# GpSimd issues the small loads of a decoder block, two column-pair counts go from 12 and 11 to 14 and 13, and the output projection's second chunk is written ahead of the first sums' eviction

## The chip, the cores and the metric

The kernel runs on one core of one Trainium2 chip. The time is the device time of one execution in microseconds, as the median over several runs; lower is better. The core has a matrix engine (TensorE, "PE", with its weight loads as "PEld"), a vector engine (DVE), a scalar engine (ACT), GpSimd (POOL), and SyncE (SP), which here issues DMAs. Matrix results are written to PSUM (8 banks of 512 float32 columns), everything else lives in SBUF.

## What is computed

One decoder layer over 256 tokens of width 2048, float32 in and out:

```
mod = silu(c) @ w_mod + b_mod          # sh1, sc1, g1, sh2, sc2, g2: 2048 each
h = rmsnorm(x, norm_mix) * (1 + sc1) + sh1
proj = h @ w_in                        # 5660 columns, cut into the inputs of four mixers
y = concat(gla, gated_deltanet, pooling, forgetting_attention)   # 512 columns each
x = x + g1 * (y @ w_out)
h = rmsnorm(x, norm_ffn) * (1 + sc2) + sh2
x = x + g2 * ((silu(conv3(h @ w_gate) + b) * (h @ w_up)) @ w_down)   # 5632 wide inside
out = rmsnorm(x, norm_final)
```

The mixers are sequence models with 4 heads of 128; the gated DeltaNet one has a causal convolution over 4 tokens, small triangular systems and a recurrence over four chunks of 64 tokens.

## The kernel before

**Numbers.** A float32 product is made from three matmuls of rounded parts. A weight tile `wr` (128 x 1024 floats, 512 KB) is loaded by SP (`load`, line 153), ACT rounds it to `wh`, DVE forms the remainder `wl = wr - wh` (`split`, line 114), and PE then multiplies high by high, high by low and low by high. There are five `wr` buffers and three each of `wh` and `wl`.

**Order.** The framework fixes the order of each engine's instructions when the program is built, from a simulated timeline, the order of the program and a few edges written by hand: `tc.issue_after(i)` keeps the instructions of its block behind `i` on the engine of `i`, and `tc.high_priority()` pulls a block forward. On the chip each engine then runs its list strictly in order, and every DMA issue is an instruction in the list of the engine that asks for it.

**Start (lines 289 to 332).** `x` is loaded as `xt`, ACT sums its squares, GpSimd takes the power -1/2, DVE scales both halves of the tokens (`tsc` at line 322), PE transposes 16 column blocks, and ACT copies them to `xnT`.

**Four groups (lines 335 to 527).** The 16 blocks of `h` (128 columns each) are made four at a time. For a group, `mods4` accumulates on DVE the shift and scale rows over 16 tiles `wm` of `w_mod` (512 KB each, five buffers, line 360), then `f` turns them into columns with tiny matmuls, forms `md` (lines 347 to 349), and ACT and DVE write the four blocks of `h`, high and low, into `HL`. While group g is multiplied, the tiles `wm` of group g + 1 are loaded and accumulated, one to a step. Group g's matrix work is `gdn(g)`, six weight tiles for the 1536 DeltaNet columns, summed in six PSUM banks `acc`, and then `extras(g)`: visits to pairs of 128-column blocks. There are 16 such pairs. A visit (`pair`, line 438) multiplies the blocks of `h` that the pair still lacks, four to a weight tile, into a bank `ext`, and adds the sum to `pr`, `gv` or `fv`. `TAKE` says how many pairs groups 0, 1 and 2 visit, counted from the end of the list; what they leave is made up later, so the number of weight tiles is the same for every `TAKE`, and a visit more costs one addition more.

**Small loads.** In group 0, after the third DeltaNet step, `rest` and `small_load` are called: SP issues 13 small loads (norms, biases, convolution weights, the masks' table `ct`) and three loads of `wsm`, 28 single columns of `w_in` as 16, 8 and 4 floats from each of 2048 rows. They stand in SP's list between the weight tiles. `rest` then transposes them, and GpSimd makes 12 masks `mk` from `ct`. `small` (the 28 columns) and `gates` come with group 3.

**Mixers (lines 546 to 943).** The pairs' remaining tiles, paced with loads of further parts of `w_mod` (`bg`: three on PE as `bgt`, three on DVE), are written so that they can run between the small operations of the four mixers, in the order GLA, pooling, attention, DeltaNet. PSUM: `ext` 2 banks, `bgt` 1, `gdt` 2, `oxt` 3.

**Output projection (lines 945 to 989).** Five chunks of columns: 512, 512, 512, 256, 256. `project(n, a)` multiplies one chunk for both halves of the tokens. Chunk 0 goes to the two `ext` banks and is written before `mx.close()`, which gives up the banks of `gdt` and `oxt`; chunks 1 to 4 go to a pool `wot` of five banks made after it. After each chunk DVE and ACT apply g1, the residual and the squares. Then come the feed-forward part (`fpt`) and the output.

Of the kernel before, what the change touches and what calls it, by code (L numbers as in the profile page):

```python
# [47 lines left out]

TAKE = (16, 12, 11)

# [23 lines left out]
def trunk_kernel(ctx: ExitStack, tc: tile.TileContext, x, c, w_mod, b_mod, norm_mix, norm_ffn, w_in,  # L74
# [24 lines left out]
    def tt(o, a, b, op):  # L99
        V.tensor_tensor(out=o, in0=a, in1=b, op=op)  # L100
# [127 lines left out]
    with ExitStack() as ph:  # L228
# [59 lines left out]
        with ExitStack() as st:  # L288
# [31 lines left out]
            G.tensor_tensor(out=ssm[:, 0:2], in0=ssm[:, 2:4], in1=mhalf[:, 0:2], op=ALU.pow)  # L320
            for t in range(NT):
                tsc(xt[:, t], xt[:, t], ssm[:, t:t + 1], None, ALU.mult)
            for k in range(0, KT, 2):
# [11 lines left out]
            def mods(g):  # L335
                for k0 in range(GROUPS[g][0], sum(GROUPS[g]), 4):
                    yield from mods4(k0, min(4, sum(GROUPS[g]) - k0))

            def mods4(k0, nk):
                n = nk * P  # L340

                def f(ga):
                    b = ext()
                    for i in range(2 * nk):
                        mm(b[:, i:i + 1], ga[:, i * P:i * P + P], ones[:, 0:1])
                    md = sp.tile([P, 2 * nk], F32, name="md", tag="md", bufs=2, padded_shape=[P, 16])
                    tt(md[:, 0:nk], b[:, 0:nk], bm(0, k0, nk), ALU.add)
                    tt(md[:, nk:], b[:, nk:2 * nk], bm(1, k0, nk), ALU.add)
                    tt(md[:, nk:], md[:, nk:], nmix[:, k0:k0 + nk], ALU.mult)
                    for kk in range(nk):  # L350
                        k = k0 + kk
                        h = sp.tile([P, T], F32, name="h", tag="h", bufs=2)
                        act(h, xnT[:, k], AF.Identity, scale=md[:, nk + kk:nk + kk + 1], bias=md[:, kk:kk + 1])
                        split(HL[:, k, 0:T], HL[:, k, T:], h)
# [3 lines left out]
                for k in range(KT):  # L358
# [6 lines left out]
                    yield  # L365

            def rest():
                nc.sync.dma_start(wlr[0:16], gla_w_lr[0])
                nc.sync.dma_start(wlr[28:29], gla_b_lr)
                nc.sync.dma_start(r2[0:48], gdn_conv[0].rearrange("j (k p) -> (j k) p", p=P))  # L370
                nc.sync.dma_start(r2[48:52], pool_scale[0].rearrange("(k p) -> k p", p=P))
                nc.sync.dma_start(r2[52:53], gla_norm)
                nc.sync.dma_start(r2[53:54], gdn_norm)
                nc.sync.dma_start(ct, cst[:, P:K_N])
                row = lambda ap: ap.partition_broadcast(P).rearrange("p o h -> p (o h)")
                nc.sync.dma_start(hrow[:, 0:4], row(gdn_a_log))
                nc.sync.dma_start(hrow[:, 4:8], row(gdn_dt_bias))
                nc.sync.dma_start(hrow[:, 8:12], row(fox_f_bias))
                nc.sync.dma_start(r3, ffn_conv_w[0, 0:2].rearrange("j (k p) -> (j k) p", p=P))
                nc.sync.dma_start(r4[0:NF], ffn_conv_w[0, 2].rearrange("(k p) -> k p", p=P))  # L380
                nc.sync.dma_start(r4[NF:], ffn_conv_b[0].rearrange("(k p) -> k p", p=P))
                b = ext()
# [13 lines left out]
            def small_load():  # L396
                nc.sync.dma_start(wsm[:, :, 0:16], wi_v[:, :, C_LR:C_LR + 16])
                nc.sync.dma_start(wsm[:, :, 16:24], wi_v[:, :, C_B:C_B + 8])
                nc.sync.dma_start(wsm[:, :, 24:28], wi_v[:, :, C_FF:C_FF + 4])  # L399
                split(wsh, wsl, wsm)  # L400

            def small():
                o = ext()[0:28, 0:T]
                for k in range(KT):
# [105 lines left out]
            for g in range(NG):  # L510
                nxt = mods(g + 1) if g < NG - 1 else iter(())
                with tc.issue_after(hold[0].ins):
# [3 lines left out]
                    for i, _ in enumerate(gdn(g)):  # L516
                        next(nxt, None)
                        if g == 0 and i == 2:
                            rest()
                            small_load()  # L520
                    if g == NG - 1:
# [3 lines left out]
                for _ in nxt:  # L525
                    pass
                hold[0] = last_wm[0]


# [15 lines left out]

        bgp = ph.enter_context(tc.tile_pool(name="bgp", bufs=1, space=PSUM))
        mx = ph.enter_context(ExitStack())
        gdp = mx.enter_context(tc.tile_pool(name="gdp", bufs=2, space=PSUM, reuse_waits="tile"))
        oxp = mx.enter_context(tc.tile_pool(name="oxp", bufs=3, space=PSUM, reuse_waits="tile"))
        dp = mx.enter_context(tc.tile_pool(name="dp", bufs=1, reuse_waits="tile"))  # L550
# [418 lines left out]

        a0 = [ext(), ext()]  # L970
        project(0, a0)
        mx.close()
        wop = ph.enter_context(tc.tile_pool(name="wop", bufs=5, space=PSUM, reuse_waits="tile"))
        x1 = bigC().rearrange("p (t d) -> p t d", t=NT)
# [3 lines left out]
        with tc.tile_pool(name="op", bufs=2, reuse_waits="tile") as op:  # L978
            for n, (c0, w) in enumerate(chunks):
                ns, gs = slice(c0, c0 + w), slice(c0 % 1024, c0 % 1024 + w)  # L980
                a = a0
                if n > 0:
                    a = [wop.tile([P, 512], F32, name="wot", tag="wot")[:, 0:w] for _ in range(NT)]
                    project(n, a)
# [158 lines left out]
```

## Time and profile before

| | before |
|---|---|
| median of 3 runs | 1299.4 us (1298.0 to 1302.43) |
| the profiled execution | 1305.52 us, of which the span is 1303.7 us |
| PE busy, share of the span | 1247.2 us, 96% |
| DVE, ACT, POOL busy | 888.9, 636.6, 23.5 us |
| read from memory | 308.51 MB |
| feed-forward matmuls (`fpt`) in the chain | 734.96 us, from 553.49 us on |

The span reaches from the first to the last instruction. The page of the profile gives busy times for each engine, the chain of work that ended last (followed back from the end), and the costliest groups of instructions. In a row of the timeline stand start, duration, engine, line, operation, output<-inputs, sizes and how many were merged; in brackets the idle time of the engine before it and what ended it. "SPq" is SP issuing a DMA. In a row of the windows stand, for each engine, busy microseconds and the number of instructions, then PEclk, the granted clock of PE (1.00 is full), the busy share of the DMA engines and their GB/s. Busy times of PE run to a modelled end, so that neighbouring matmuls overlap; how tightly they are packed is read from a stretch's length divided by their number.

### The profile page before, as it was taken

How to read it: one execution, taken by the hardware profiler on the slowest of the kernel's cores; microseconds unless marked ns; L12 is line 12 of the kernel's file. 1: busy time of each engine (PE TensorE's matmuls, PEld its weight loads, DVE VectorE, ACT ScalarE, POOL GpSimd, SP SyncE). 2: the span in 40 equal slices, each digit the busy share in tenths (PEclk: the TensorE clock that was granted, in tenths of full speed). 3: DMA queues.
4: the chain of work that ended last, by engine and by line, in shares of the span. 5: the costliest groups of instructions: out<-in, count | busy, mean ns of one | idle time of the engine just before them, and what ended most of it. 6: DMA issues, size and time to landing. Idle time of an engine off the chain costs nothing.

```text
span 1303.7 us, 19845 instructions
## 1 busy us (share of the span) xinstructions
PE 1247.2 (96%) x7663; PEld 1078.8 (83%) x7663; DVE 888.9 (68%) x1201; ACT 636.6 (49%) x1000; POOL 23.5 (2%) x31
## 2 busy tenths in 40 slices
PE   2799999999999999999999999999999999999995
PEld 1699999898976687888888888888888888888884
DVE  7578797989763387676666656665756687974543
ACT  3455344674364454555555545554555553443432
POOL 0200000010000000000000000000000000000000
PEclk8799999999999999999999999999999999999998
DMA  9999998796557888656666666657666699875662
GB/s 329 270 367 377 320 335 295 250 336 224 174 200 255 311 315 286 176 148 190 180 196 192 180 197 190 190 165 211 190 184 175 208 353 381 306 258 188 194 193 82
DMA packets 168597, 311.91 MB, mean 239 GB/s; under 512 B 16172, under 2 KB 54067, under 8 KB 167863
## 3 DMA queue, kind: packets, MB, share of 16 engines
q1 hardware_dynamic: 168503, 310.65, 72.9%
q8 instruction: 60, 0.98, 0.3%
q14 instruction: 34, 0.28, 0.1%
HBM read 308.51 MB, written 2.10 MB: 238 GB/s over the span
## 4 chain that ended last, share of the span: by engine, by line
PE 91%; DMA 4%; DVE 1%; SPq 1%; ACT 1%; issue 1%; POOLq 0%; ACTq 0%; DVEq 0%
PE fpt L97 56%; PE ext L97 16%; PE wot L97 5%; PE gdt L97 4%; PE acc L97 4%; DMA wm<-in_w_mod_dram 4%; PE bgt L97 3%; PE oxt L97 2%; DMA wr<-in_w_in_dram 1%; DVE ga L103 1%; ACT xT L1011 0%; DVE m L100 0%; DVE wl L100 0%; SPq L399 0%; PE oxt L873 0%
## 5 line engine op out<-in xcount | busy, mean ns | idle before, releaser
L100 DVE TENSOR_TENSOR wl<-wr,wh 128x1024 fp32r<-128x1024 f32 x384 | 469.0, 1222 | 296.8 <-ACT wh L115 296.1
L115 ACT CAST wh<-wr 128x1024 fp32r<-128x1024 f32 x384 | 403.5, 1051 | 490.2 <-PE fpt L97 314.9
L97 PE MATMUL fpt<-bigA,wh 128*128 128x512 f32 x1408 | 399.3, 395 | 2.1 <-DVE bigA L103 2.1
L97 PEld LDWEIGHTS fpt<-bigA,wh 128*128 128x128 f32 x1408 | 239.0, 188 | 32.8 <-issue 2.2
L97 PEld LDWEIGHTS fpt<-bigA,wl 128*128 128x128 f32 x1408 | 222.8, 189 | 34.5 <-DVE wl L100 3.7
L97 PE MATMUL fpt<-bigA,wl 128*128 128x256 f32 x1408 | 240.7, 279 | 0.0
L103 DVE SCALAR_TENSOR_TENSOR ga<-wm,cond,ga 128x1024 f32<-128x1024 f32 x139 | 177.9, 1280 | 14.1 <-DMA wm<-in_w_mod_dram 13.2
L97 PE MATMUL ext<-bigA,wh 128*128 128x256 f32 x768 | 138.4, 282 | 0.0
L97 PE MATMUL fpt<-wl,AH 128*128 128x512 f32 x352 | 137.5, 391 | 0.0
L97 PE MATMUL fpt<-wh,AL 128*128 128x512 f32 x352 | 137.0, 389 | 0.0
L97 PE MATMUL fpt<-wh,AH 128*128 128x512 f32 x352 | 123.4, 390 | 0.0
L97 PEld LDWEIGHTS ext<-bigA,wh 128*128 128x128 f32 x768 | 118.5, 190 | 3.1 <-DVE E L100 0.8
L97 PE MATMUL ext<-bigA,wl 128*128 128x256 f32 x384 | 107.9, 281 | 1.7 <-DVE wl L100 1.7
L97 PEld LDWEIGHTS fpt<-wl,AH 128*128 128x128 f32 x352 | 66.1, 188 | 14.3 <-DVE wl L100 0.4
L97 PEld LDWEIGHTS fpt<-wh,AH 128*128 128x128 f32 x352 | 66.1, 188 | 14.1 <-ACT wh L115 0.2
L97 PEld LDWEIGHTS fpt<-wh,AL 128*128 128x128 f32 x352 | 66.1, 188 | 14.0 <-issue 0.2
L97 PEld LDWEIGHTS ext<-bigA,wl 128*128 128x128 f32 x384 | 72.9, 190 | 2.9 <-DVE wl L100 1.9
L97 PE MATMUL acc<-bigA,wh 128*128 128x256 f32 x384 | 68.7, 285 | 5.6 <-ACT bigA L115 3.2
L97 PE MATMUL ext<-wh,bigA 128*128 128x256 f32 (+1 forms) x320 | 69.3, 308 | 0.0
L97 PEld LDWEIGHTS acc<-bigA,wh 128*128 128x128 f32 x384 | 59.7, 195 | 6.0 <-ACT bigA L115 3.3
L97 PE MATMUL wot<-wh,bigA 128*128 128x512 f32 (+1 forms) x256 | 63.0, 337 | 0.0
L97 PEld LDWEIGHTS ext<-wh,bigA 128*128 128x128 f32 x320 | 52.9, 192 | 5.5 <-issue 1.4
(340 smaller groups left out, 1193.2 us busy)
## 6 DMA issues: line engine op xcount, KB each, us to landing
wm<-in_w_mod_dram SPq DMA_DIRECT2D x192, 512.0 KB, 5.6
wr<-in_w_in_dram SPq DMA_DIRECT2D x88, 512.0 KB, 9.1
wr<-in_ffn_w_gate_dram SPq DMA_DIRECT2D x88, 512.0 KB, 3.7
wr<-in_ffn_w_up_dram SPq DMA_DIRECT2D x88, 512.0 KB, 4.3
wr<-in_ffn_w_down_dram SPq DMA_DIRECT2D x88, 512.0 KB, 4.6
wr<-in_w_out_dram SPq DMA_DIRECT2D x32, 512.0 KB, 4.2
xt<-in_x_dram SPq DMA_DIRECT2D x2, 1024.0 KB, 7.1
bigC<-in_x_dram SPq DMA_DIRECT2D x2, 1024.0 KB, 9.1
```

What stands on the lines that cost most here:

```text
L97: PE.matmul(o, lhsT=l, rhs=r, start=start, stop=stop, skip_group_check=True)
L100: V.tensor_tensor(out=o, in0=a, in1=b, op=op)
L103: V.scalar_tensor_tensor(out=o, in0=a, scalar=s, in1=b, op0=op0, op1=op1)
L115: S_.copy(hi, src)
```

## The change

- `TAKE` is (16, 14, 13) in place of (16, 12, 11).
- The scaling of `xt` goes from two DVE instructions of 2048 columns to four ACT instructions of 1024, both first halves first.
- The 13 loads of `rest` and the three of `small_load` are issued by GpSimd in place of SP, behind the multiplication that finishes `md` of group 1, and that multiplication itself goes from DVE to GpSimd. The rest of `rest` is written after group 2, and the splitting of `wsm` into `small`.
- Output chunk 1 is written before `mx.close()`, into two `oxt` banks, whose pool now stays open; `wot` has two banks, and chunks 2, 3 and 4 use `wot`, `ext` and `oxt`.

```diff
-TAKE = (16, 12, 11)
+TAKE = (16, 14, 13)
...
-            for t in range(NT):
-                tsc(xt[:, t], xt[:, t], ssm[:, t:t + 1], None, ALU.mult)
+            for hs in (slice(0, D // 2), slice(D // 2, D)):
+                for t in range(NT):
+                    act(xt[:, t, hs], xt[:, t, hs], AF.Copy, scale=ssm[:, t:t + 1])
...
-                    tt(md[:, nk:], md[:, nk:], nmix[:, k0:k0 + nk], ALU.mult)
+                    if k0 == GROUPS[1][0]:
+                        asked[0] = G.tensor_tensor(out=md[:, nk:], in0=md[:, nk:], in1=nmix[:, k0:k0 + nk], op=ALU.mult)
+                    else:
+                        tt(md[:, nk:], md[:, nk:], nmix[:, k0:k0 + nk], ALU.mult)
...
+            def rest_load():
+                G.dma_start(wlr[0:16], gla_w_lr[0])
...
             def rest():
-                nc.sync.dma_start(wlr[0:16], gla_w_lr[0])
...
             def small_load():
-                nc.sync.dma_start(wsm[:, :, 0:16], wi_v[:, :, C_LR:C_LR + 16])
-                nc.sync.dma_start(wsm[:, :, 16:24], wi_v[:, :, C_B:C_B + 8])
-                nc.sync.dma_start(wsm[:, :, 24:28], wi_v[:, :, C_FF:C_FF + 4])
+                for o, c, n in ((0, C_LR, 16), (16, C_B, 8), (24, C_FF, 4)):
+                    G.dma_start(wsm[:, :, o:o + n], wi_v[:, :, c:c + n])
+
+            def small():
                 split(wsh, wsl, wsm)
-
-            def small():
...
-                        if g == 0 and i == 2:
-                            rest()
-                            small_load()
...
                 hold[0] = last_wm[0]
+                if g == 0:
+                    with tc.issue_after(asked[0].ins):
+                        small_load()
+                        rest_load()
+                if g == 2:
+                    rest()
...
         bgp = ph.enter_context(tc.tile_pool(name="bgp", bufs=1, space=PSUM))
+        oxp = ph.enter_context(tc.tile_pool(name="oxp", bufs=3, space=PSUM, reuse_waits="tile"))
         mx = ph.enter_context(ExitStack())
         gdp = mx.enter_context(tc.tile_pool(name="gdp", bufs=2, space=PSUM, reuse_waits="tile"))
-        oxp = mx.enter_context(tc.tile_pool(name="oxp", bufs=3, space=PSUM, reuse_waits="tile"))
...
-        a0 = [ext(), ext()]
-        project(0, a0)
+
+        sums = [[new() for _ in range(NT)] for new in (ext, oxt)]
+        for n in range(2):
+            project(n, sums[n])
         mx.close()
-        wop = ph.enter_context(tc.tile_pool(name="wop", bufs=5, space=PSUM, reuse_waits="tile"))
+        wop = ph.enter_context(tc.tile_pool(name="wop", bufs=2, space=PSUM, reuse_waits="tile"))
+        wot = lambda: wop.tile([P, 512], F32, name="wot", tag="wot")
...
-                a = a0
-                if n > 0:
-                    a = [wop.tile([P, 512], F32, name="wot", tag="wot")[:, 0:w] for _ in range(NT)]
+                if n < 2:
+                    a = sums[n]
+                else:
+                    a = [(wot, ext, oxt)[n - 2]()[:, 0:w] for _ in range(NT)]
                     project(n, a)
```

More of the change, by code (lines that the diff above doesn't have):

```diff
@@ L337, in mods @@
                     yield from mods4(k0, min(4, sum(GROUPS[g]) - k0))
+            asked = [None]
             def mods4(k0, nk):
@@ L365, in mods4 @@
                     yield
-            def rest():
-                nc.sync.dma_start(wlr[0:16], gla_w_lr[0])
[L369 to L381, printed above, removed]
+            def rest_load():
+                G.dma_start(wlr[0:16], gla_w_lr[0])
+                G.dma_start(wlr[28:29], gla_b_lr)
+                G.dma_start(r2[0:48], gdn_conv[0].rearrange("j (k p) -> (j k) p", p=P))
+                G.dma_start(r2[48:52], pool_scale[0].rearrange("(k p) -> k p", p=P))
+                G.dma_start(r2[52:53], gla_norm)
+                G.dma_start(r2[53:54], gdn_norm)
+                G.dma_start(ct, cst[:, P:K_N])
+                row = lambda ap: ap.partition_broadcast(P).rearrange("p o h -> p (o h)")
+                G.dma_start(hrow[:, 0:4], row(gdn_a_log))
+                G.dma_start(hrow[:, 4:8], row(gdn_dt_bias))
+                G.dma_start(hrow[:, 8:12], row(fox_f_bias))
+                G.dma_start(r3, ffn_conv_w[0, 0:2].rearrange("j (k p) -> (j k) p", p=P))
+                G.dma_start(r4[0:NF], ffn_conv_w[0, 2].rearrange("(k p) -> k p", p=P))
+                G.dma_start(r4[NF:], ffn_conv_b[0].rearrange("(k p) -> k p", p=P))
+            def rest():
                 b = ext()
```

## The prediction

> **What bounds the kernel now.** I read the page first, then the chain in order of time, then a table of windows cut at the stages that the chain shows, and then what PE, SP and DVE do in the first 80 us. The page:
>
> ```profile
> PE 1247.2 (96%) x7663; PEld 1078.8 (83%) x7663; DVE 888.9 (68%) x1201; ACT 636.6 (49%) x1000; POOL 23.5 (2%) x31
> ...
> PE 91%; DMA 4%; DVE 1%; SPq 1%; ACT 1%; issue 1%; POOLq 0%; ACTq 0%; DVEq 0%
> ```
>
> PE is busy for 96% of the span and makes 91% of the chain. So PE's own work is the floor, and a change can give back only time in which PE waits or is not packed. Three pieces of the chain give the packed pace (start, length, what):
>
> ```profile
> 137.16 31.98 PE ext L97 x278
> 478.34 36.17 PE wot L97 x158
> 553.49 734.96 PE fpt L97 x3875
> ```
>
> 278 matmuls of 256 columns in 31.98 us are 0.115 us each, 158 of 512 columns in 36.17 us 0.229. The last piece, 735 us of feed-forward matmuls without a hole, the change does not touch. The windows, by stage (then some short stretches):
>
> ```profile
> core 0: us, PE busy (x) PEld busy (x) DVE busy (x) ACT busy (x) POOL busy (x), PEclk, DMA share, GB/s
> 42.27:76.60 34.33, 29.18 (x220) 28.21 (x220) 21.52 (x21) 14.53 (x23) 7.27 (x12) 0.90 0.93 281
> 76.60:116.20 39.60, 39.56 (x329) 39.43 (x330) 32.56 (x34) 22.98 (x34) 0.00 (x0) 0.96 1.07 372
> 116.20:169.10 52.90, 51.21 (x451) 51.02 (x450) 43.22 (x46) 21.56 (x24) 0.00 (x0) 1.00 0.99 332
> 169.10:223.50 54.40, 54.40 (x467) 53.94 (x466) 49.29 (x55) 23.79 (x30) 0.00 (x0) 1.00 0.96 327
> 246.00:460.00 214.00, 211.91 (x1571) 169.07 (x1570) 143.28 (x258) 109.41 (x247) 10.54 (x7) 0.98 0.75 254
> ```
> ```profile
> 42.20:52.60 10.40, 10.33 (x74) 10.01 (x75) 4.29 (x7) 4.36 (x11) 7.27 (x12) 0.83 0.64 83
> 56.00:59.50 3.50, 3.00 (x14) 3.00 (x15) 2.33 (x3) 1.31 (x3) 0.00 (x0) 0.51 1.04 393
> 74.30:76.60 2.30, 0.31 (x3) 0.10 (x1) 2.29 (x2) 1.53 (x2) 0.00 (x0) 0.99 1.08 365
> 76.60:80.00 3.40, 3.36 (x16) 3.36 (x17) 2.83 (x3) 1.14 (x2) 0.00 (x0) 0.51 1.07 368
> 298.40:301.80 3.40, 3.40 (x18) 3.40 (x17) 2.99 (x7) 0.00 (x0) 0.00 (x0) 0.50 0.02 6
> 448.60:452.00 3.40, 3.40 (x18) 2.55 (x17) 1.22 (x1) 3.29 (x12) 0.00 (x0) 0.50 1.04 395
> ```
>
> At 0.115 us each, the 220 matmuls of 42.27 to 76.60 need 25.3 us and take 34.3: 9.0 lost. The 329 of the next row need 37.8 of 39.6: 1.8 lost. The 451 of 116.20 to 169.10 need 51.9 of 52.9: 1.0 lost. So the first group loses 10.8 us; the groups after it are nearly packed, and 246 to 460 shows PE busy for 211.9 of 214.
>
> Why the first group loses time:
>
> ```profile
> 42.27 1.65 PE L97 MATMUL acc<-bigA,wh 128*128 128x256 f32 x6 [3.17 <-ACT bigA L115]
> 55.24 0.50 PE L97 MATMUL acc<-bigA,wh 128*128 128x256 f32 x2 [2.40 <-ACT wh L115]
> 56.50 0.58 PE L97 MATMUL acc<-bigA,wl 128*128 128x256 f32 x1 [0.76 <-DVE wl L100]
> ```
> ```profile
> 30.09 0.77 SPq L155 DMA_DIRECT2D wr<-in_w_in_dram  x1
> ...
> 43.83 0.40 SPq L397 DMA_DIRECT2D wsm<-in_w_in_dram  x1
> 44.27 2.12 SPq L398 DMA_DIRECT2D wsm<-in_w_in_dram  x1
> 46.43 2.73 SPq L399 DMA_DIRECT2D wsm<-in_w_in_dram  x1
> 49.21 1.20 SPq L155 DMA_DIRECT2D wr<-in_w_in_dram  x1
> ```
> ```profile
> DMA packets 7207, 1.24 MB, mean 104 GB/s; under 512 B 6698, under 2 KB 6883, under 8 KB 7205
> ```
>
> SP has three weight tiles issued by 30.9 us and asks for the fourth only at 49.21; in between stand the small loads. From 40 to 52 us the DMA engines move 1.24 MB, 104 GB/s, against 372 in the row of 76.60 to 116.20. PE runs dry at 52.6 and waits 2.40 and 0.76 us; the granted clock is at 0.51 from 56.00 to 59.50. From there PE eats tiles as fast as they land, until it runs dry again at 74.3 and has 0.51 once more from 76.60 to 80.00.
>
> **The change, part by part.**
>
> *Small loads off SP's list.* The fourth to sixth weight tiles and the `wm` tiles among them no longer stand behind 16 small issues. A step of `gdn` needs one weight tile and one `wm` tile, 1.05 MB; at 372 GB/s that is 2.82 us, and its 24 matmuls take 24 x 0.115 = 2.76. PE starts with three tiles landed, about 6 us ahead, and loses 0.06 us a step on the 16 steps that carry a `wm`: it does not run dry. Of the 10.8 us, what stays is the cold start: from 42.20 to 52.60 there were 74 matmuls, 8.5 us at full pace, in 10.4, so 1.9. Gain 8.9 us.
>
> The Trainium skill, DMA: Bandwidth & Descriptors, section "Issuing engines are not separate DMA queues", says that DMAs asked for by any engine run on the same 16 DMA engines, and that asking from several saves only the sequencer's time to start them, usually little beside the transfer. By it alone the move would be worth little; the 104 GB/s of this trace say that here the start was what was scarce. Its first half is weighed below as "given back".
>
> *Scaling `xt` on ACT.*
>
> ```profile
> 13.45 2.47 DVE L107 TENSOR_SCALAR xt<-xt,ssm 128x2048 f32<-128x2048 f32 x2
> ...
> 34.12 1.28 DVE L103 SCALAR_TENSOR_TENSOR ga<-wm,cond,ga 128x1024 f32<-128x1024 f32 x1 [0.75 <-DMA wm<-in_w_mod_dram]
> ```
> ```profile
> 21.11 5.58 DMA wm<-in_w_mod_dram
> ...
> 28.10 5.93 DMA wm<-in_w_mod_dram
> ```
> ```profile
> 6.62 1.91 ACT L112 ACTIVATE pr<-xt 128x2048 f32<-128x2048 f32 x1 [2.10 <-DMA xt<-in_x_dram]
> ```
>
> The chain alternates between a `wm` buffer given back by DVE and the load into it (21.11 and 28.10). Without the 2.47 us of scaling DVE gives buffers back up to 2.4 us earlier. Whether memory then delivers as much earlier no row shows: bounds 0 and 2.4, and I take 1.7, nearer the upper end, because the loads at 21.11 and 28.10 start from a returned buffer. On ACT the scaling is four instructions of about 1 us each (half of 1.91), 4 us in all; its product, `h`, reaches PE at 42.27, so it is covered. If that cover were gone it would cost 4 less 2.47, 1.5 us.
>
> *`md` of group 1 on GpSimd.*
>
> ```profile
> 100.18 0.16 DVE L100 TENSOR_TENSOR md<-md,V 128x4 f32<-128x4 f32 x1
> ```
> ```profile
> 44.11 7.83 POOL L393 TENSOR_SCALAR mk<-ct 128x128 uint8<-128x128 f32 x12 [31.59 <-DMA ct<-in_cst_dram]
> 224.84 1.46 POOL L813 MEMSET Sg<- 128x512 f32 x3 [172.90 <-DVE bigA L100]
> ...
> 367.75 1.01 POOL L839 TENSOR_TENSOR ls<-ls,mhalf 128x4 f32<-128x4 f32 x1 [69.47 <-DVE s L100]
> ```
> ```profile
> 116.04 0.39 PE L97 MATMUL acc<-bigA,wh 128*128 128x256 f32 x2
> ```
>
> 0.16 us becomes about 1.0 (a GpSimd operation of the same size, the last of these GpSimd rows). `md` is ready at 100.3 and PE turns to group 1 at 116.04; with PE 10 us earlier `md` moves as well, since its tiles are no longer held up. Nothing on the path. What waits behind it on GpSimd is only the new DMAs.
>
> *Where the small loads go.* They start near 90 us. Their takers are ACT's cast of `wsm`, with every later weight cast queued behind it, then PE:
>
> ```profile
> 218.72 0.40 PE L97 MATMUL ext<-bigA,wsh 128*28 128x256 f32 x2
> ```
> ```profile
> 51.64 0.57 ACT L115 CAST wsh<-wsm 128x448 fp32r<-128x448 f32 x1 [4.39 <-DMA wsm<-in_w_in_dram]
> ```
>
> SP took from 43.83 to 51.64 for the three loads of `wsm`, 7.8 us; here there are some 125 us. GpSimd's speed at it no row shows: bounds 0 and the rival below. The transfers themselves take DMA time: share 0.64 over 10.4 us in the row of 42.20 is 6.7 us, moved to where the share was 1.07. In the new order the first two groups ask for 22 + 20 weight tiles and 32 `wm`, 38.8 MB, 104 us at 372 GB/s, between 28 and 160 us, so there is room: 0 (to 6.7). What else `rest` does (three transposes, ACT's small copies, 7.83 us of masks) moves behind group 2; ACT is busy 23.8 of 54.4 us there, GpSimd is idle, and the masks are first read in the mixers: 0, and 7.8 if the masks were waited for.
>
> *`TAKE`.* Four weight tiles, 4 x 24 x 0.115 = 11.0 us of PE, go from the mixer stage to groups 1 and 2, 5.5 each. PE's sum is unchanged. DVE gets per group two splits and two additions more:
>
> ```profile
> L100 DVE TENSOR_TENSOR wl<-wr,wh 128x1024 fp32r<-128x1024 f32 x19 | 22.9, 1218 | 1.9 <-ACT wh L115 1.8
> L100 DVE TENSOR_TENSOR pr<-ext,pr 128x512 f32<-128x512 f32 x7 | 4.8, 687 | 4.9 <-PE ext L97 4.9
> ```
>
> 2 x 1.22 + 2 x 0.69 = 3.8 us, in 5.5 us more of PE time. In the fuller group, the second, DVE goes from 49.3 of 54.4 to 53.1 of 59.9: covered. The 1.0 us lost in group 1 I count as gained, for its stall was a late `wl` and DMA is less pressed (0 to 2).
>
> *The mixer stage* has 11 us less to fill with and, at its end, three quarters of output chunk 1 instead, which do not need DeltaNet: 72 matmuls of 0.229, 16.5 us. But there are few holes: PE idles 2.1 us (214.0 less 211.9), and two dips of the clock, at 298.40 and 448.60, cost 1.7 each. Best case -5.5. Worst case the chain of DeltaNet keeps its length and the 11 us stay as holes. Since PE is packed now, DeltaNet's small matmuls stand behind filling ones, so that chain shortens as filling goes: I take 0.
>
> *Output chunk 1 earlier*: 22 us of matmuls (96 x 0.229) change place only. Chunks 3 and 4 now wait for evictions of chunks 0 and 1, two chunks back: 0.
>
> **Sum.** 8.9 + 1.7 + 1.0 = 11.6 us. The profiled execution took 1305.5 us (span 1303.7, 1.8 around it), which is 6.1 above the median of 1299.4; so about 1293.9 in a like profile, and 1287.8 in the median.
>
> **Rivals.** *Mixers left unfilled*: DeltaNet's chain is bound by its own latency, and the 11 us come back as holes: 1298.8. For it: the clock dips at 448.60, where little but DeltaNet is left. Against: PE is busy throughout. Chance 0.11.
>
> *Given back*: the small transfers cost their 6.7 us later, because DMA is the bound of groups 0 and 1 (shares 1.07 and 0.99): 1294.5. Against: PE loses only 1.8 and 1.0 us there now. Chance 0.12.
>
> *Slower: `wsm` comes late.* If GpSimd makes the 6144 short rows so slowly that they land after about 215 us, ACT stands at its cast, and with it the weight casts of group 3 and PE. It decides from 125 us on, 16 times SP's 7.8; from 137 us (125 + 11.6) the kernel is slower than before, and at 150 us the 25 us of wait give 1313. Against: GpSimd has nothing else to do from 51.9 to 224.8 us, and the masks, 7.8 us of the same list, come after. Chance 0.07. The Trainium skill, SBUF — State Buffer, section "Who interferes with whom", gives a way to it: an operation of DVE in a two-port mode shuts GpSimd out, so that it cannot write its descriptors. No run here shows it yet; the DVE operations of these stages are nearly all of the kinds that the page does not count among those.
>
> *The loads aren't what starves PE*: if DVE or DMA alone set the first group, only 1.7 to 3 us come: 1297. Against: the 104 GB/s. Chance 0.05.
>
> **Numbers.** The forecast has 0.65, the rivals 0.35. A measurement of this kernel can tell about 0.3% from no change, 3.9 us: faster is under 1295.5. The forecast and *given back* are faster, 0.77; *mixers left unfilled* and *aren't what starves PE* the same, 0.16; slower 0.07. Range: low 1299.4 - (8.9 + 2.4 + 2 + 5.5) = 1280.6; high, 1298.8 of the unfilled mixers: 1280.5 to 1299.
>
> **What would show it.** Right: SP issues weight tiles without a break from 28 to 60 us, DMA above 330 GB/s from 40 to 52, no PE wait at 52 or 74, clock 1.00 from about 46 on; first `acc` matmul near 40.6 and group 1 near 105.5 (116.04 - 10.6); `wsm` landed well ahead of the cast; PE busy all through the mixers, and `fpt` 11 to 12 us earlier. Wrong: PE idle in the mixers, GpSimd still issuing after 200 us, or stalls behind weight tiles between 90 and 130.

## The result and the profile after

| | before | after |
|---|---|---|
| median of 7 runs each | 1299.84 us (1298.0 to 1302.43) | 1303.96 us (1301.9 to 1305.68) |
| profiled execution (its span) | 1305.5 (1303.7) | 1302.6 (1300.8) |
| feed-forward matmuls begin, in the profiled execution | 553.49 us | 551.70 us |

The ratio is 1.0025, 95% interval 1.0013 to 1.0036: the change makes the kernel slower by 2 to 5 us. The forecast was 12 us faster. The profiled execution of before lies 5.7 us above its kernel's median and that of after 1.4 below, so the two traces must not be compared by their ends; a second profile of before (run *same_again*, span 1300.8) stands beside them below.

The start went as forecast. Windows of after, PE only; the columns are busy PE (number of matmuls), granted clock, DMA share, GB/s:

```profile
core 0: us, PE busy (x), PEclk, DMA share, GB/s
40.00:60.00 20.00, 20.00 (x174) 0.97 1.07 372
60.00:80.00 20.00, 20.00 (x175) 1.00 1.07 368
...
90.00:95.00 5.00, 5.00 (x45) 1.00 1.11 221
...
105.00:110.00 5.00, 1.17 (x7) 0.95 1.01 367
110.00:115.00 5.00, 5.00 (x33) 0.71 1.05 387
```

174 and 175 matmuls in 20 us are the packed pace of 0.115 us: no wait at 52 or 74 us, no dip of the clock after the cold start (which ends at 41.2 us and makes the 0.97), the DMA engines at 370 GB/s. PE even begins earlier than forecast, at 38.36 us (42.27 in before, forecast 40.6), and turns to group 1 at 102.3 (116.0 in before, forecast 105.5). The first row of the groups in after:

```profile
38.36 1.86 PE L97 MATMUL acc<-bigA,wh 128*128 128x256 f32 x7 [2.00 <-ACT bigA L115]
```

Then something is given back. At 90 to 95 us the DMA engines are as busy as ever (1.11) and move only 221 GB/s, and at 105 to 110 PE has 7 matmuls in 5 us. The chain of after and its DMA view from 85 to 105 us say why:

```profile
91.19 16.02 DMA wr<-in_w_in_dram
107.28 1.05 ACT wh L115
```
```profile
q1 hardware_dynamic: 3421, 4.97, 86.4%
q0 software_dynamic: 525, 0.80, 20.9%
```

One weight tile takes 16.02 us from its issue to its landing. In those 20 us GpSimd's queue (q0) holds a fifth of the engines' time for 0.80 MB. The Trainium skill, DMA: Bandwidth & Descriptors, section "Issuing engines are not separate DMA queues", says that whoever asks, the same 16 engines work; the trace agrees. Against the packed pace PE loses 5.6 us between 100 and 120 us (before lost 1.6 us between 120 and 140, which is gone).

What matters more comes after the groups. These are rows of the timeline of before and then of after: the last DeltaNet column of the groups (`acc`), the recurrence's three steps (`kti`), and DeltaNet's last matmuls (`Y`).

```profile
240.91 0.28 PE L97 MATMUL acc<-bigA,wl 128*128 128x256 f32 x1
...
426.36 1.16 PE L97 MATMUL gdt<-bigC,kti 64*128 64x128 f32 x8
433.21 1.16 PE L97 MATMUL gdt<-bigC,kti 64*128 64x128 f32 x8
438.78 1.16 PE L97 MATMUL gdt<-bigC,kti 64*128 64x128 f32 x8
...
462.17 0.60 PE L735 MATMUL gdt<-ident,Y 128*128 128x128 f32 x4
```
```profile
241.57 0.28 PE L97 MATMUL acc<-bigA,wl 128*128 128x256 f32 x1
...
427.07 1.16 PE L97 MATMUL gdt<-bigC,kti 64*128 64x128 f32 x8
435.21 1.16 PE L97 MATMUL gdt<-bigC,kti 64*128 64x128 f32 x8
449.09 1.16 PE L97 MATMUL gdt<-bigC,kti 64*128 64x128 f32 x8
...
474.84 0.60 PE L746 MATMUL gdt<-ident,Y 128*128 128x128 f32 x4
```

The groups end where they did, with 11 us more matmul work in them: so the start's gain is there. That this matches the forecast to a microsecond is luck: the start won some 3 us more than forecast, and the stall near 105 us took 5.6 that were not in the sum. But the mixer stage, which has those 11 us less to do, is not shorter. The recurrence begins 0.7 us later than in before, its third step comes 13.9 us after the second in place of 5.6 (39 matmuls of output chunk 0, 8.9 us, which the list now places there, stand between), and DeltaNet ends 12.7 us later. Windows of after and of *same_again*:

```profile
340.00:480.00 140.00, 134.98 (x824) 0.96 0.78 270
```
```profile
340.00:480.00 140.00, 139.81 (x926) 1.00 0.73 256
```

PE was busy for 139.8 of 140 us and is now for 135.0. If for each pair of neighbouring matmuls the time between their starts is taken, less the packed pace (0.115 us up to 256 columns, 0.229 for 512, 0.245 for `bgt`), the sum is what PE lost, by waits, by a low clock or by loose packing: 4.7 us in before and 15.7 in after for 340 to 480 us. This sum is called the loss below. In the mixer stage it is good to about 1 us, as it depends on how the smallest matmuls are counted.

### The profile page after: what moved, and what is told of

Same layout as the page of the kernel before. It is cut to its first block, busy times and chain, and to the rows that moved or that the text cites. A ratio compares the mean times of both kernels' runs of the same rounds, so it can differ in the third digit from the quotient of the medians.

```text
span 1300.8 us, 19881 instructions
## 1 busy us (share of the span) xinstructions
PE 1247.4 (96%) x7663; PEld 1074.1 (83%) x7663; DVE 890.1 (68%) x1202; ACT 642.5 (49%) x1004; POOL 37.4 (3%) x48
## 4 chain that ended last, share of the span: by engine, by line
PE 92%; DMA 3%; DVE 2%; ACT 1%; issue 1%; SPq 0%; POOLq 0%; ACTq 0%; POOL 0%; DVEq 0%
PE fpt L97 56%; PE ext L97 16%; PE acc L97 5%; PE oxt L97 5%; PE gdt L97 4%; PE bgt L97 3%; DMA wm<-in_w_mod_dram 2%; PE wot L97 2%; DVE ga L103 2%; DMA wr<-in_w_in_dram 1%; ACT xT L1026 0%; DVE wl L100 0%; ACT wh L115 0%; DVE m L100 0%; ACT h L112 0%
## 5 line engine op out<-in xcount | busy, mean ns | idle before, releaser
L103 DVE SCALAR_TENSOR_TENSOR ga<-wm,cond,ga 128x1024 f32<-128x1024 f32 x139 | 178.0, 1281 | 11.7 <-DMA wm<-in_w_mod_dram 10.1
L97 PE MATMUL ext<-bigA,wh 128*128 128x256 f32 x768 | 135.0, 279 | 0.0
L97 PE MATMUL ext<-wh,bigA 128*128 128x256 f32 (+1 forms) x384 | 79.5, 300 | 0.0
L97 PEld LDWEIGHTS ext<-wh,bigA 128*128 128x128 f32 x384 | 61.4, 188 | 3.7 <-ACT wh L115 0.8
L97 PE MATMUL ext<-wl,bigA 128*128 128x256 f32 (+1 forms) x192 | 57.5, 300 | 0.0
```

The costliest lines, as they stand in the source:

```text
L97: PE.matmul(o, lhsT=l, rhs=r, start=start, stop=stop, skip_group_check=True)
L103: V.scalar_tensor_tensor(out=o, in0=a, scalar=s, in1=b, op0=op0, op1=op1)
```

## The experiments

All are compared with before, timed beside it. "Stage" is the time from the last `acc` matmul to the first transposes ahead of the feed-forward part, in the profiled execution. It is one execution of each kernel: before itself has 305.6 us (groups end at 240.9) and 301.1 in *same_again*, so differences under 5 us in this column say little by themselves.

| run | median, us | before, us | ratio, 95% interval | groups end | stage |
|---|---|---|---|---|---|
| after | 1303.96 | 1299.84 | 1.0025 (1.0013, 1.0036) | 241.6 | 303.1 |
| same_again | 1300.74 | 1300.36 | 1.0001 (0.9985, 1.0016) | 241.3 | 301.1 |
| start_only | 1302.31 | 1300.36 | 1.0017 (1.0002, 1.0033) | 232.4 | 311.1 |
| take_only | 1321.09 | 1300.36 | 1.0153 (1.0128, 1.0178) | 251.3 | 308.3 |
| out_only | 1301.03 | 1300.36 | 1.0002 (0.9989, 1.0015) | 239.7 | 302.6 |
| no_take | 1301.59 | 1300.68 | 1.0013 (0.9998, 1.0027) | 232.5 | 310.8 |
| no_out | 1309.97 | 1300.68 | 1.0065 (1.0049, 1.0081) | 242.9 | 312.7 |
| rates | 1298.90 | 1300.68 | 0.9988 (0.9977, 0.9999) | 244.0 | 300.1 |
| no_fill | 1282.54 (one run) | 1300.68 | | 238.7 | 286.4 |
| take_rates | 1313.39 | 1300.32 | 1.0096 (1.0081, 1.0111) | 250.4 | 303.9 |
| rates_no_take | 1302.04 | 1300.32 | 1.0013 (1.0000, 1.0026) | 233.5 | 313.4 |
| rates_up | 1309.80 | 1300.32 | 1.0072 (1.0059, 1.0086) | 242.0 | 308.8 |
| late_loads | 1297.12 | 1300.32 | 0.9977 (0.9965, 0.9990) | 240.4 | 296.5 |
| skip2 | 1300.22 | 1301.16 | 0.9989 (0.9976, 1.0002) | 234.7 | 308.9 |
| skip4 | 1303.78 | 1301.16 | 1.0027 (1.0013, 1.0041) | 228.3 | 317.0 |
| late_no_take | 1302.33 | 1301.16 | 1.0002 (0.9987, 1.0016) | 232.0 | 311.3 |
| late_no_out | 1298.44 | 1301.16 | 0.9979 (0.9968, 0.9991) | 240.7 | 298.8 |
| half_stream | 1297.28 | 1300.56 | 0.9974 (0.9963, 0.9984) | 228.3 | 307.6 |
| more_room | 1306.69 | 1300.56 | 1.0058 (1.0039, 1.0077) | 232.8 | 317.4 |

Counted at the packed pace, the matmuls of this stage need 298.6 us with the old pairs and 287.6 with the new ones. That is a floor: *same_again* lies 2.5 us above it, before 7.0, *late_loads* 8.9, *start_only* 12.5, after 15.6 and *skip4* 18.4.

### One part at a time

*same_again* is before itself.

> The kernel before, once more, for what the comparison itself can tell and for a second look at its first 140 us. Theory 1 (the start's gain is real and is spent later): time within 0.3% of before, and TensorE again loses about 10 us against its packed pace between 40 and 80 us and 1 to 2 us between 120 and 140. Rival (the profiled execution of before, 1305.5 us against a median of 1299.8, was a poor one at the start, so that there was less to gain): the loss between 40 and 80 us comes out at 5 us or less.

Measured: the loss between 40 and 80 us is 10.1 us, and 1.6 at 120 to 140. There was as much to gain as the profile of before showed; the rival falls.

*start_only* has the loads on GpSimd and the scaling on ACT, and nothing else.

> Only the two edits at the start: the small loads asked for by GpSimd behind group 1's md, and xt scaled on ScalarE; the pairs stay at 16, 12, 11 and the output projection stays as before. Theory 1: the loss between 40 and 80 us goes (about 10 us), some 5.6 us come back near 105 us while the short-row loads hold the DMA engines and weight tiles queue behind them (against 1.6 us at 120 to 140 in before), and the mixers are as in before: 6 to 8 us less than before, about 1292 to 1294. Rival (there was little to gain): within 2 us of before. Third reading (the mixers lose their 11 us from the start's edits themselves): about 4 us slower than before, and the loss stands between 340 and 480 us.

Measured: 2.0 us slower in the medians, none of the three expectations whole; the time is the rival's, but not for its reason, as there was much to gain. The start does what was forecast: the loss at 40 to 80 us is 1.0, and the groups end 8.9 us earlier (the second fence is *start_only*, the first *same_again*; in each the SP rows show a run of `wm` loads and the first `w_out` load behind it):

```profile
383.55 56.24 SPq L185 DMA_DIRECT2D wm<-in_w_mod_dram  x30
439.84 5.01 SPq L155 DMA_DIRECT2D wr<-in_w_out_dram  x5
```
```profile
379.38 61.31 SPq L185 DMA_DIRECT2D wm<-in_w_mod_dram  x31
440.74 5.01 SPq L155 DMA_DIRECT2D wr<-in_w_out_dram  x5
```

The 8.9 us do not arrive: SP gets to `w_out` at 440.74 in place of 439.84. They are gone between 240 and 380 us, where the loss is 11.9 us against 1.0 in *same_again*. A part of it is the clock. Windows of *start_only*, then of *same_again*:

```profile
350.00:360.00 10.00, 10.00 (x67) 0.82 0.86 298
360.00:370.00 10.00, 10.00 (x57) 0.84 0.22 71
```
```profile
350.00:360.00 10.00, 10.00 (x82) 1.00 0.14 47
360.00:370.00 10.00, 10.00 (x72) 1.00 0.93 319
```

With 0.18 and 0.16 missing from full clock, PE spent 6.8 us at half speed, which costs 3.4; another such stretch of 3.4 us at 288 us costs 1.7. (The first profile of before has two such stretches of 3.4 us in this stage too, at 298 and 449 us; *same_again* has none.)

*take_only* has `TAKE = (16, 14, 13)` alone.

> Only the pairs of columns: 16, 14, 13 in place of 16, 12, 11. Theory 1a (the mixers are left without filling by the pairs that the groups took): the groups end up to 11 us later, less what they fill of idle time, and the mixer stage does not get shorter: 8 to 11 us slower, and the loss between 340 and 480 us grows from about 4.7 to about 15 us. Theory 1b (the mixer loss is due to the second output chunk between DeltaNet's steps): the mixers get shorter by what the groups get longer, within 2 us of before, loss between 340 and 480 us about 5 us.

Measured: 20.7 us slower, more than either expected. The groups end 10.0 us later, which is the 11 us moved into them; and the stage, with 11 us less matmul work, is 7 us longer instead of shorter. The recurrence's steps are drawn apart as in after:

```profile
437.59 1.16 PE L97 MATMUL gdt<-bigC,kti 64*128 64x128 f32 x8
444.37 1.16 PE L97 MATMUL gdt<-bigC,kti 64*128 64x128 f32 x8
459.28 1.16 PE L97 MATMUL gdt<-bigC,kti 64*128 64x128 f32 x8
477.56 0.66 PE L735 MATMUL gdt<-ident,Y 128*128 128x128 f32 x4 [2.43 <-ACT Y L112]
480.59 1.25 PE L735 MATMUL gdt<-ident,Y 128*128 128x128 f32 x4 [2.38 <-ACT Y L112]
```

Output chunk 0 is done first as far as it goes without DeltaNet; when DeltaNet then ends, nothing is left to lay between its last steps, and PE waits 2.43 and 2.38 us.

*out_only* has the output chunk alone.

> Only the output projection: its second 512 columns are multiplied in the mixer stage too, with the PSUM pools that this needs. Theory 1a (the mixers' loss comes of the pairs): 0 to 5 us faster than before, DeltaNet's last work at 453 to 463 us as in before. Theory 1b (the second chunk's matmuls and loads stand ahead of DeltaNet's steps and delay them): DeltaNet's end moves out by up to 10 us and the time grows by 3 to 11 us.

Measured: no difference (0.9989 to 1.0015), DeltaNet's end at 458 us. The late DeltaNet of after comes with the pairs, not with the chunk.

### Two parts at a time, and the pacing

*no_take* sets the pairs back in after; *no_out* sets the output projection back.

> The changed kernel with the pairs set back to 16, 12, 11. Alone, the start's edits gave +2.0 us (1302.3 against 1300.4), the output chunk +0.7, the pairs +20.7, and all together +4.1: they do not add up. Theory 1 (the pairs taken out of the mixer stage leave it unfilled): the mixer stage is filled again and 7 to 11 us come back, 1291 to 1295. Rival (the order of the mixer stage's list, which is laid out anew by the simulated timeline for every variant, is what the start's 9 us are lost in, with or without the pairs): like the start's edits alone, 1299 to 1305.

> The changed kernel with the output projection as before: start and pairs alone. The pairs alone cost 20.7 us, of which at most 11 are matmul time not put to use; in that run the four steps of DeltaNet's recurrence stretch over 23 us with output chunk 0 written between them, in before over 13. Theory 1 (the pairs, whatever the rest): 1313 to 1320, as the start takes nothing off the mixers. Rival (order of the list): anything between 1300 and 1320, without the stretched recurrence where it is near the lower end. Third reading (the early second chunk repairs what the pairs spoil): slower than the changed kernel by 5 us or more.

Measured: *no_take* 1301.6, as the rival said. *no_out* 1310.0, 6 us slower than after: this fits the third reading, that the early second chunk does fill holes, but only such as the pairs have made. The parts do not add up: 2.0, 20.7 and 0.7 alone, 4.1 together.

The mixer stage hands out the tiles of `w_mod` at so many for each filling step. With the new pairs there are 21 steps in place of 25. *rates* scales the two numbers:

```diff
-ON_PE, PE_RATE = "s0 s1 h0", 0.38
+ON_PE, PE_RATE = "s0 s1 h0", 0.45
-ON_DVE, DVE_RATE = "h1 g0 g1", 0.69
+ON_DVE, DVE_RATE = "h1 g0 g1", 0.82
```

> The changed kernel with the pacing of the mixer stage scaled to its fewer filling steps: the tiles of w_mod are handed out at 0.38 (on TensorE) and 0.69 (on VectorE) a filling step, 25 steps before and 21 with the new pairs; here 0.45 and 0.82, so that as many are handed out by the end of the steps as before. Theory pacing (with fewer steps, w_mod tiles are left over that come after DeltaNet's operations in the program and fill its last part badly): the loss between 340 and 480 us falls from 15.7 to about 5 us, and the time to about 1293. Theory 1 (there is simply 11 us too little to fill with): the same time as the changed kernel, 1302 to 1306.

Measured: 1298.9, 5 us less than after, half of what the pacing theory asked. From the first `kti` to DeltaNet's last row it takes 34.6 us, as in before (35.8); in after it was 47.8. The loss at 340 to 480 us falls to 5.1, as that theory said; but 7.1 us are lost at 280 to 300, where in *rates* PE is not busy for 3.2 us and the clock is at half for 10:

```profile
280.00:300.00 20.00, 16.75 (x110) 0.81 0.77 262
```

*take_rates* puts the same pacing beside the pairs alone, *rates_no_take* beside the other parts, and *rates_up* goes further (0.55 and 1.0).

> The kernel before with the pairs 16, 14, 13 and the pacing scaled to them (0.45 and 0.82). The pairs alone took 1321.1 us against 1300.4; there the time from the recurrence's first matmul to DeltaNet's last was 43.8 us (34.9 in before). With the changed kernel the same scaling took that time from 48.1 to 34.7 us and the whole from 1304.0 to 1298.9. Theory pacing (what the pairs spoil is the hand-out of w_mod tiles, so that DeltaNet's last part is mixed with output chunk 0): that time falls to about 35 us and 9 us or more come back, 1312 or less. Theory 1 (11 us of matmul time went into the groups, and the mixers cannot shrink, whatever the pacing): stays above 1311. Both may hold, each with its part: then about 1311.

> The changed kernel with the pairs at 16, 12, 11 and the pacing at 0.45 and 0.82. Without the new pacing it took 1301.6 us: its groups end 9 us earlier than in before (232.5 us), and from there to DeltaNet's last matmul it takes 228 us in place of 217, so that the 9 us are lost between 232 and 423 us. Theory order (the list of the mixer stage, laid out anew for each variant, decides, and a small change of the pacing changes it): the stage's length moves by 5 us or more either way, and the time with it. Rival (something that is there whatever the order, DeltaNet's chain or the transfers, ends at about 423 us): the recurrence begins at 420 to 426 us again and the time is 1300 to 1303.

> The changed kernel with still faster pacing: 0.55 and 1.0. At 0.38 and 0.69 it took 1304.0 us, at 0.45 and 0.82 1298.9. Theory pacing as such (the sooner the w_mod tiles are handed out, the less is left beside DeltaNet's last part): 1298 or less. Rival (0.45 was a lucky order): 1300 to 1306.

Measured: *take_rates* 1313.4, which is 7.7 us less than *take_only*, and 13.1 more than before. That is nearest to the third reading, that both hold: some 8 us of the 20.7 go with the pacing, and the other 13 are about the 11 us of matmul time that went into the groups and were not gained back. *rates_no_take* 1302.0, with the recurrence at 421 us once more. *rates_up* 1309.8, above both expectations: sooner is not better; 0.45 is near an optimum, or a good order among many. With three settings tried, that scaling by the steps is the reason why 0.45 is better is argued and not shown.

### Does the mixer stage depend on matmul time at all?

*no_fill* leaves out the filling of the mixer stage.

```diff
-        ex = extras(NG - 1)
+        def unfilled():
+            for p in range(len(pairs)):
+                for _ in range(done[p], NG):
+                    yield
+                done[p] = NG
+
+        ex = unfilled()
```

> The kernel before without the 25 weight tiles of the pairs that are left to the mixer stage: their loads, roundings and 600 matmuls (69 us of TensorE) are left out, so that DeltaNet and the other mixers work on sums that lack them. In before 217 us pass from the last DeltaNet column's matmul (241 us) to DeltaNet's last matmul (458). Theory latency (DeltaNet's own chain of small operations sets the end of the mixers, so that matmul time taken out of the stage is not gained): at least 190 of the 217 us stay. Rival (TensorE's list sets it; what counts is how the filling lies between the small operations): about 150 us.

Measured: 69 us of matmuls less, and the kernel is 18 us faster (one run). DeltaNet's last matmuls, in rows of *no_fill*:

```profile
238.67 0.28 PE L97 MATMUL acc<-bigA,wl 128*128 128x256 f32 x1
...
450.95 1.10 PE L735 MATMUL gdt<-ident,Y 128*128 128x128 f32 x4 [0.95 <-ACT Y L112]
```

213 us (450.95 and 1.10 less 238.67) against 217 in *same_again*. The stage as in the table is 14.7 us shorter; beside the 4 us, that is output chunk 0, of which 48 matmuls more (11 us) were done by DeltaNet's end. So little of the 69 us came through. But where the rest went is not DeltaNet's latency alone, which the expectation would have it be. The same stretch of *no_fill* as a window, PE only, columns as above:

```profile
238.67:452.05 213.38, 186.91 (x1079) 0.86 0.75 258
```

PE is not busy for 26.5 us, and a clock of 0.86 in place of 1.00 costs up to another 30 (0.14 of 213; less where PE waits anyway). So of the time that was taken out, about as much came back with a slow clock as came back as waits. Nor are the waits DeltaNet's alone: of the chain that ended last from 236 to 460 us, `bgt` matmuls make 17.0%, the loads of `wm` 14.6% and the `gdt` matmuls, with DeltaNet's among them, 16.3%. What the run shows is that matmul time taken out of this stage is mostly not gained; it does not tell DeltaNet's chain, the stream of `w_mod` and the clock apart.

*skip2* and *skip4* turn the question round: they shorten the groups of before and leave the mixer stage's work alone.

```diff
+SKIP = 4
...
                 for p in ps:
-                    yield from pair(p, done[p], g + 1)
+                    if g > 0 or p >= SKIP:
+                        yield from pair(p, done[p], g + 1)
                     done[p] = g + 1
...
-                    add(dst, a, g0 == 0, scale)
+                    add(dst, a, g0 == (p < SKIP), scale)
```

> The kernel before without two of the 16 visits of group 0: two weight tiles, 48 matmuls, 5.5 us of TensorE, are left out, so that two pairs' sums lack group 0's part; the mixer stage has the same work as in before. If the mixer stage starts earlier and ends earlier with it (rival: order alone eats the start's gain): 5 to 6 us faster, 1295. If the stage has an end that stays (theory of a fixed end, as the recurrence's beginning at 421 to 424 us in six kernels suggests): 1299 to 1301.

> The same with four visits of group 0 left out, 11 us of TensorE. Passing through: 1289 to 1291. Fixed end: 1299 to 1301. Order that changes with every variant: between the two, and not in proportion to the run with two.

Measured: 1300.2 and 1303.8. Eleven microseconds of matmuls taken out of the groups make the kernel 2.6 us slower. The table shows the same in all the kernels with the old pairs, the whole filling and the whole stream, but for *more_room*: the groups end anywhere from 228.3 to 241.3 us, and the stage ends (the two columns added) between 542 and 547 us. Here SP's list of *skip4*:

```profile
372.12 59.27 SPq L186 DMA_DIRECT2D wm<-in_w_mod_dram  x27
433.69 0.80 SPq L978 DMA_DIRECT2D bigC<-in_x_dram  x2
436.00 9.53 SPq L186 DMA_DIRECT2D wm<-in_w_mod_dram  x5
445.87 1.40 SPq L156 DMA_DIRECT2D wr<-in_w_out_dram  x3
```

DeltaNet ended early, at 440 us, but `w_out` is asked for only behind the run of `wm` loads, at 445.87; PE has 33 matmuls from 440 to 453 us. Such a run ahead of the first `w_out` load takes 56 to 70 us for 27 to 32 tiles in 17 of the profiles, and it waits for PE. The waits of SP in *start_only* from 232 to 460 us:

```profile
SPq L185 <- PE bgt L97: 77.1, 27, 12.8
SPq L185 <- DVE ga L103: 32.5, 15, 4.5
SPq L185 <- DMA wm<-in_w_mod_dram: 19.2, 11, 4.1
```

77.1 us go to waiting for one of four buffers that a `bgt` matmul has to give back, and that matmul stands in PE's list between DeltaNet's steps.

*half_stream* and *more_room* test this, both from *late_no_take* (below).

```diff
-            wms = []
-            for kk in range(2):
+            if not pst or k % 4 == 0:
+                wms = []
+            for kk in range(2 - len(wms)):
```

> late_no_take (1302.3 us: the groups end at 232 us, and the mixer stage gives the 9 us back) with every second pair of w_mod tiles for TensorE not loaded: its matmuls read the pair before once more, so that the same matmuls, sums and small operations stay and 24 of 48 loads (12.6 MB) and their waits for buffers are left out; the vectors s2 and the first half of sh2 are then not the reference's. Theory stream (w_mod's tiles through four buffers, each behind the one before on SP, set the end of the mixer stage): the first w_out load comes 8 us or more ahead of 438.9 us and the time is 1290 to 1295. Rival (order of the small operations alone): 1299 to 1305, with the recurrence's beginning at 420 to 424 us as before.

> late_no_take with the third job of w_mod tiles for TensorE (h0, 16 tiles) loaded into the five buffers of wr, which stand empty between the pairs' end at 380 us and the first w_out load at 439 us. Theory stream: the tiles of 380 to 440 us come faster, the first w_out load moves forward by 4 us or more, and the time falls to 1294 to 1298. Rival (order alone): 1299 to 1305. If half_stream gains and this does not, it is the number of loads and not the room for them.

Measured: *half_stream* 1297.3, between the two: 5 us less than *late_no_take* by the medians, with intervals that do not overlap (in the profiles the groups, which the edit does not touch, end 3.7 us earlier and the stage is 3.7 us shorter, less than two profiles of before differ by). SP gets to `w_out` 32 us earlier:

```profile
370.54 36.04 SPq L186 DMA_DIRECT2D wm<-in_w_mod_dram  x16
406.62 12.52 SPq L155 DMA_DIRECT2D wr<-in_w_out_dram  x8
```

But DeltaNet still ends at 458 us, as in *same_again*, with a loss of 10.8 us at 440 to 460, of which a half clock from 451.3 to 458.1 us makes 3.4. So the stream seems to hold up some of the stage, and not all of it. The result lies below the rival's range and above the theory's, and a new order of the list may have had a part in the 5 us; that DeltaNet's chain is what comes close behind is argued and not shown. *more_room* is slower by 4 us: with the third job in `wr`'s buffers `w_out` had to wait for them and was asked for at 447.4. It says nothing of the stream as such. More buffers of its own for `w_mod` were not tried.

### The loads a group later

*late_loads* is *rates* with the small loads behind group 2's `md`; *late_no_out* is the same with the output projection of before; *late_no_take* has the old pairs and the old pacing.

```diff
-                    if k0 == GROUPS[1][0]:
+                    if k0 == GROUPS[2][0]:
...
-                if g == 0:
+                if g == 1:
```

> The changed kernel with the pacing 0.45 and 0.82 and the small loads one group later: GpSimd asks for them behind group 2's md in place of group 1's. With them behind group 1's md TensorE lost 5.4 us between 100 and 120 us, while the DMA engines moved 221 GB/s at 90 to 95 us with a busy share over 1. Theory 'the short rows take the engines' time wherever they stand': the stall moves to about 160 to 180 us and has the same 3 to 6 us; the time is the same within 2 us. Rival (there is slack in the later group, where the share was 0.80 to 0.85 between 200 and 240 us): the loss at 100 to 120 goes and 2 us or less come later, 1294 to 1297.

> The changed kernel with the pairs at 16, 12, 11, the pacing as it was, and the small loads behind group 2's md. With the loads behind group 1's md it took 1301.6 us. Theory 'take the stall away and the gain shows': 4 to 5 us less, 1297. Theory of a fixed end of the mixer stage: 1300 to 1302, with the recurrence's beginning at 420 to 424 us again though the groups end near 229.

> The best variant so far (pacing 0.45 and 0.82, small loads behind group 2's md: 1297.1 us) with the output projection as in before. In no run so far has the early second chunk filled a gap that was seen (alone: +0.7 us, 0.0002 of the time, not to be told from nothing). Theory 'the chunk does nothing': 1296 to 1299. Rival (it fills what is left at DeltaNet's end when the pairs are 14 and 13, as the changed kernel without it took 1310.0 against 1304.0): 1302 or more.

Measured: *late_loads* 1297.1, the fastest of the kernels that leave nothing out, 0.23% under before. The first fence is *rates*, the second *late_loads*:

```profile
100.00:120.00 20.00, 17.15 (x129) 0.91 1.05 364
180.00:200.00 20.00, 20.00 (x177) 1.00 1.07 374
```
```profile
100.00:120.00 20.00, 20.00 (x179) 1.00 1.07 375
180.00:200.00 20.00, 18.88 (x153) 1.00 1.06 366
```

The stall at 105 us is gone; about half of it comes back at 180 to 200. *late_no_take* is the same as before: what the start's edits win is lost in the mixers with the late loads too. *late_no_out* is the same as *late_loads* within the intervals: once the pacing is right, the second chunk is worth nothing.

## Why the prediction was wrong, step by step

**Small loads off SP's list, and scaling on ACT** (8.9 and 1.7): right in the groups, where they end 8.9 us earlier in *start_only*, and the second is mis-sized. PE begins 3.9 us earlier than in before, where the upper bound was 2.4: DVE now accumulates 15 tiles in 20.26 us without a wait, so memory did deliver earlier.

**Where the small loads go** (0, to 6.7): mis-sized. It cost 5.6 us near 105 us. My ground, that there was room over the whole of groups 0 and 1, was a mean over 130 us; PE needs the tile that is queued now. In the medians the move of the stall brought *late_loads* only 1.8 us, with intervals that overlap. The 1.0 us of the late `wl` in group 1 did come back.

**`TAKE`** (PE's sum unchanged): true and beside the point. 11 us went into the groups, and *take_only* with *take_rates* show that they were not gained in the mixers.

***The mixer stage* (0) is the step that failed**, and with it the line of the sum that carried the groups' gain to the end unchanged. By the forecast this stage is 11.0 us shorter. In the profiles it is 303.1 us against 305.6 and 301.1 in the two of before, and as the groups ended where the forecast had them, nearly all of the 15.7 us between forecast and result lie here. The matmuls did become fewer, 287.6 us at the packed pace in place of 298.6; but the loss rose from 2.5 or 7.0 us to 15.6, where I had put no change.

My ground was that PE was busy for 211.9 of 214 us, so that PE's work set the length, and that DeltaNet's chain "shortens as filling goes". The first half holds as a floor: *same_again* stands 2.5 us above it. It does not say that a shorter list would be packed as well, and the runs show that it is not. *take_only* and *take_rates* show that the 11 us come back as lost time; *rates*, that some 5 us of what after lost go with the pacing numbers, which were left as they stood for 25 steps and which the prediction does not mention. *start_only* and *skip4* show that a stage with its own work untouched gets longer by about as much as it begins earlier (10.0 for 8.9 us and 15.9 for 13.0, against *same_again*), so that the start's 9 us do not pass either. *no_fill* shows that of 69 us of filling little is gained.

The worst case that I named, 11 us as holes, was the rival *mixers left unfilled*, with 0.11 and 1298.8. It was right that the 11 us come back; that DeltaNet's own latency is why is not shown, and it too let the start's gain through.

***Given back*** was right about its place (a stall behind weight tiles between 90 and 130 us) and near in size (5.6 us for 6.7), and ***`wsm` comes late*** wrong: the cast of `wsm` ran at 103 us, far ahead of its use.

**Output chunk 1** (0): right; *out_only* and *late_no_out* show no difference. It matters only beside the pairs with the old pacing, *no_out*.

**What stays open.** The order of the mixer stage is laid out anew for every variant. In *start_only* the loss of 11.9 us at 240 to 380 us is shown, and the clock accounts for 5 of it; which placement of which operation makes the rest is not shown. Why the stage ends at nearly the same time wherever the groups end is open too. *half_stream* speaks for a part of the stream of `w_mod` in it, *skip4* shows that `w_out`'s loads behind that stream can come after DeltaNet's end; how much is DeltaNet's chain and how much the clock no run separates.

## What to carry to other kernels

An engine that is busy throughout a stage gives a floor for it, and no promise that the stage shrinks with the work, if the list was tuned to fill the waits of a chain: before moving work out of such a stage, leave it out once and see whether the stage gets shorter, and read the granted clock beside it, which may fall. Constants that pace one kind of work by the steps of another (here 0.38 and 0.69 a filling step) belong in the same edit that changes the number of steps, as numbers to be tried again. And when small loads are moved, put them by the transfers that are queued at that moment, not by the mean load of the stage.

## What the chip showed that was not expected

**The clock halves while PE is counted as busy.** Windows of *start_only*, then of *no_fill*, cut at the change of the clock; in neither stretch does the view of waits list one for PE:

```profile
356.40:363.20 6.80, 6.80 (x23) 0.50 0.63 229
363.20:366.60 3.40, 3.40 (x26) 1.00 0.50 154
```
```profile
271.40:291.90 20.50, 20.50 (x82) 0.50 0.58 201
291.90:295.30 3.40, 3.40 (x31) 1.00 0.86 276
```

Counted as busy for the whole of 6.8 and 20.5 us, PE runs at 0.50. Ahead of the first stretch, from 353.0 to 356.4 us, begin 27 matmuls, of 256 columns (6), 128 (5) and 1 (16), whose columns fill under a third of the time at the packed pace; ahead of the second, from 268.0 to 271.4 us, begin 23 whose columns fill about a quarter. So filling seems to be worth more than its own time, as it keeps the clock up for such matmuls. It is no sharp rule: *same_again* has 3.4 us as thin at 361 us (27 matmuls) and keeps its clock. The Trainium skill, TensorE: Matmul & The Clock Gate, section "Part 1: The HAM clock gate (the "warmup" mystery)", ties the half clock to idle windows of about 3.4 us; the lengths agree (6.8 and 20.5 are 2 and 6 such windows), but here it was not idleness as the profile counts it. That it is the columns in a window that count is my reading and was not tested.

**Small loads slow the large ones beside them.** While GpSimd's 0.80 MB were under way, SP's own queue moved 4.97 MB in 86.4% of 20 us, 288 GB/s of its engines' time; at 40 to 60 us it moved 7.42 MB in 106.4%, 349 GB/s. Moving the small loads off SP's list freed the list; it did not free the engines.
